# Residual inputs on VectorE in pieces, squares and row rests by products, and a written order at the norm and the routing of a two-layer MoE transformer kernel

## The chip, the cores and the metric

The kernel runs on one core of one Trainium2 chip. The metric is the device time of one execution in microseconds (us). TensorE (PE) does the products, VectorE (DVE), ScalarE (ACT) and GpSimd (POOL) the rest. SyncE (SP) issues nearly all weight transfers on one queue. Each engine takes its own instructions in a fixed order and waits at one until what it needs is there.

## The reference

256 tokens of width 1024 pass through two layers. Cut to what matters here:

```python
# layer 1: modulated conformer convolution, then a mixture of experts
y = depthwise_conv(glu(h @ w_in + b_in), w_dw)        # 31 taps
y = silu(layernorm(y, ln_g, ln_b)) @ w_out
x = x + gate1 * y
h = rmsnorm(x) * (1 + scale2) + shift2
x = x + gate2 * hier_moe(h)                           # 32 experts, top 2 of one group of 8
x = rmsnorm(x, final_g)
# layer 2: latent attention, layer norm, block attention, final norm
x = layernorm(x + mla(x), ln_g, ln_b)
...
```

The residual input of the latent attention is therefore the normalized row times `final_g` (called x3 here), and that of the block attention is the normalized row times `ln_g` plus `ln_b` (called x4).

## The kernel before, in words

Tokens stand in two tiles of 128 rows (t = 0, 1), channels in eight chunks of 128 (k). A product with float32 accuracy is made of single-pass ones: a value is split into a rounded part (suffix h) and a rest (suffix l), hi by ACT and lo by DVE (`split`, L282 and L283), and three products are summed.

**Convolution and its norm (L457 to L585).** DVE does the taps of four chunks (L411), PE those of the other four as products with small blocks. After each chunk `chunk_stats` takes off a first estimate of the mean (`mp`), squares on ACT, and adds up the squares of six chunks on POOL into `ssum` (L484); the chunks' values go into `asum` (L471), also on POOL. PE makes the mean per token (`pms`) and the sums per token (`pst`) of these by products with a column of 1/1024. From `pst` come variance, the power -0.5 on POOL (L565), a diagonal `rst`, and its spread over all partitions by a product (`prs`). Each chunk is then centred (L573), scaled (L577), passed through SiLU (L579, `ysl`) and split into `yh`, `yl` for the out-projection `po`. Beside it lie the two halves of the first gate: products `adp`, copied out by ACT as `ads` (L297). The out-projection's weights are split into `wh`, `wl` by ACT and DVE.

**Routing (L683 to L780).** The rows `x2` get their norm factor `rs2`; a rounded part `xh` and a rest `xl` are made of them, the rest of one tile by POOL, that of the other by DVE (L745). DVE finds the experts by a chain of small operations, two exponentials of it on ACT. `pw` are products that keep PE busy and whose result is not used. A gather by products (`acc`) starts the experts. The 32 experts' weights come in pieces of 2 MB (`in_moe`), issued by SP as buffers become free.

**Layer 2.** In the latents' stage POOL multiplies the rows by `final_g` (L1455, two operations of 128x1024), while DVE splits weights. After the layer norm `to_channels` turns `x4n` into channels chunk by chunk: PE transposes (`pt`), ACT or DVE scales (`xf`), ACT rounds (`xh`), DVE takes the rest (`xl`, 128x128). POOL makes x4 at the same time (L1546 and L1547, four operations of 128x1024). Then `values(0)`, and eight key chunks: PE makes a chunk, `rope_t` splits it (`cqh`), turns it by a product, DVE and POOL multiply by sine and cosine (`t`, `raw`), and DVE adds them (`kn`).

Where a pool's scheduler places an instruction, it goes by due times; `keep_in_program_order` and `pe_order` pin an instruction to its place in the source among the others so pinned on its engine, and `issue_after` places the ones inside it behind a given one.

Of the kernel before, what the change touches and what calls it, by code (L numbers as in the profile page):

```python
# [6 lines left out]
F32 = mybir.dt.float32  # L7
# [41 lines left out]
LN_DVE = ()  # L49
# [29 lines left out]
WARM_R = 2, 3  # L79
# [106 lines left out]
def build(tc, A, out, dbg=None, stop=None):  # L186
# [79 lines left out]
    crep = pre.tile([P, KD, 32], F32, name="crep")  # L266
    modc = const.tile([P, 48], F32, name="modc")
# [21 lines left out]
    def ada_part(psp, pool, ps=None):  # L289
        w = W.get()  # L290
        pt = psp.tile([P, 512], F32, name="adp", tag="adp")
        for k in range(KD):
            j = k % 4
            mm(pt[32 * j:32 * j + 32, :], crep[:, k, :], w[:, k, :], k < 4, k >= 4)
        if ps is None:
# [169 lines left out]
    ssum = wk.tile([P, T], F32, name="ssum", tag="ssum", bufs=1)  # L465
# [11 lines left out]
    def chunk_stats(i, k):  # L477

        nc.vector.tensor_sub(y[:, k, :], y[:, k, :], mp)
        if i < 6:  # L480
            s2 = ssum if i == 0 else wk.tile([P, T], F32, name="s2", tag="sg")
            nc.scalar.activation(s2, y[:, k, :], AF.Square)
            if i:
                nc.gpsimd.tensor_add(ssum, ssum, s2)  # L484
            if i >= PRE:
                running_sum(i, asum, y[:, k, :], PRE)
        if i == 5:
            mm(pms, mean1, asum, True, False)
            products(2, asum, False)
            products(0, ssum, False)  # L490
        elif i > 5:
            s2 = wk.tile([P, T], F32, name="s2", tag="sg")
            nc.scalar.activation(s2, y[:, k, :], AF.Square)
# [24 lines left out]
    for group in CONV:  # L518
# [4 lines left out]
        for k in group:  # L523
# [27 lines left out]
    def rows_of(w, k):  # L551

        wh = wsp.tile([P, 512], F32R, name="wh", tag="wh")
        wl = wsp.tile([P, 512], F32R, name="wl", tag="wl")
        split(wh, wl, w[:, k, :])
        return wh, wl

    wo = W.peek(wo_at - W.nget)
    wos = [rows_of(wo, k) for k in range(WSP)]
    del wo  # L560

    nc.vector.tensor_copy(st[:, 0:4], pst)
    nc.vector.tensor_mul(st[:, 2:4], st[:, 2:4], st[:, 2:4])
    nc.vector.scalar_tensor_tensor(st[:, 0:2], st[:, 0:2], EPS, st[:, 2:4], op0=OP.add, op1=OP.subtract)
    nc.gpsimd.tensor_tensor(out=st[:, 0:2], in0=st[:, 0:2], in1=expn[:, 0:2], op=OP.pow)  # L565
    rst = wk.tile([P, T], F32, name="rst", tag="mp", bufs=1)
    for t in range(NT):
        nc.vector.tensor_scalar(rst[:, P * t:P * t + P], ident, st[:, t:t + 1], None, op0=OP.mult)
# [3 lines left out]
    for k in range(KD):  # L572
        nc.vector.tensor_sub(y[:, k, :], y[:, k, :], pms)  # L573
    yh = xy.tile([P, KD, T], F32R, name="yh", tag="up")
    yl = xt.tile([P, KD, T], F32R, name="yl")
    for k in range(KD):
        nc.vector.tensor_mul(y[:, k, :], y[:, k, :], prs)  # L577
        ys = wk.tile([P, T], F32, name="ysl", tag="ht")
        nc.scalar.activation(ys, y[:, k, :], AF.Silu, scale=vec[:, V_LNG + k:V_LNG + k + 1],  # L579
                             bias=vec[:, V_LNB + k:V_LNB + k + 1])  # L580
        if k in LN_DVE:
            nc.vector.tensor_copy(yh[:, k, :], ys)
            nc.vector.tensor_sub(yl[:, k, :], ys, yh[:, k, :].bitcast(F32))
        else:
            split(yh[:, k, :], yl[:, k, :], ys)  # L585
# [83 lines left out]
    for h in range(2):  # L669
        ada_row(5, h, g2b[:, 512 * h:512 * h + 512], psA)  # L670
# [42 lines left out]
    def first_max(val, n, mx, oh, tmp):  # L713
# [31 lines left out]
    tc.keep_in_program_order(nc.vector.scalar_tensor_tensor(  # L745
        xl2[:, 0, :], x2[:, 0, :], rs2[:, 0:1], xh2[:, 0, :].bitcast(F32), op0=OP.mult, op1=OP.subtract))
# [5 lines left out]
    for i in range(WARM_R[1]):  # L752
        mm(pw[:, 0:256], ident, g2b[:, 0:256], True, True)
    del pw
# [47 lines left out]


    ig = mo.tile([P, P + 4 * E], F32R, name="ig")
    nc.scalar.copy(ig[:, 2 * E:2 * E + P], ident)
    for t in range(NT):
        c = (P + 2 * E) * t
        nc.scalar.copy(ig[:, c:c + E], G[:, t, :])
        nc.vector.tensor_sub(ig[:, c + E:c + 2 * E], G[:, t, :], ig[:, c:c + E].bitcast(F32))
# [463 lines left out]
    def rope_t(dst, pin, rot, cos, sin):  # L1273
# [289 lines left out]
    for m in range(8):  # L1563
        rope_t([kn[:, m, :]], chunk_t(KD, xh, xl), r64, tab(T_COSB), tab(T_SINB))
# [124 lines left out]
```

## Time and profile before

| | |
|---|---|
| time, median of 3 runs (lowest to highest) | 946.23 us (945.17 to 946.7) |
| the profiled execution | 945.95 us |
| its span, first to last instruction | 944.3 us |
| mean granted clock of PE, as a share of full speed | 0.981 |
| PE busy | 869.0 us (92%) |
| DVE busy | 526.6 us (56%) |
| ACT busy | 361.2 us (38%) |
| POOL busy | 58.2 us (6%) |
| read from HBM | 287.34 MB |

The shares are averages over the whole span. Between the profiled execution and its span lie 1.65 us. Read by stages, there are stretches in which PE waits and stretches in which the transfers are what ends last; the rows further down show both.

### The profile page before, as it was taken

How to read it: one execution, taken by the hardware profiler on the slowest of the kernel's cores; microseconds unless marked ns; L12 is line 12 of the kernel's file. 1: busy time of each engine (PE TensorE's matmuls, PEld its weight loads, DVE VectorE, ACT ScalarE, POOL GpSimd, SP SyncE). 2: the span in 40 equal slices, each digit the busy share in tenths (PEclk: the TensorE clock that was granted, in tenths of full speed). 3: DMA queues.
4: the chain of work that ended last, by engine and by line, in shares of the span. 5: the costliest groups of instructions: out<-in, count | busy, mean ns of one | idle time of the engine just before them, and what ended most of it. 6: DMA issues, size and time to landing. Idle time of an engine off the chain costs nothing. (4 is left out here: it accounts for less than half of the span.)

```text
span 944.3 us, 15434 instructions
## 1 busy us (share of the span) xinstructions
PE 869.0 (92%) x6227; PEld 609.6 (65%) x6227; DVE 526.6 (56%) x1243; ACT 361.2 (38%) x788; POOL 58.2 (6%) x62
## 2 busy tenths in 40 slices
PE   4899879899999999999699999878999996999996
PEld 1597346665565555656356555538988874988975
DVE  2699965623343333334223342357777868758876
ACT  1455645412122121212012121145766735655761
POOL 0000210100000000000000000003100004110112
PEclk9899989999999999999899999999999998999998
DMA  9994968789999999999999999974432441624211
GB/s 372 411 389 191 406 249 317 323 362 426 427 427 428 426 427 426 427 426 430 422 428 425 426 429 425 425 311 159 170 140 91 179 178 45 255 102 179 90 45 45
DMA packets 23580, 289.44 MB, mean 307 GB/s; under 512 B 2736, under 2 KB 3408, under 8 KB 6096
## 3 DMA queue, kind: packets, MB, share of 16 engines
q1 hardware_dynamic: 21872, 282.29, 72.4%
q10 hardware_dynamic: 1632, 6.11, 1.8%
q8 instruction: 51, 0.84, 0.4%
q14 instruction: 25, 0.20, 0.1%
HBM read 287.34 MB, written 1.05 MB: 305 GB/s over the span
## 5 line engine op out<-in xcount | busy, mean ns | idle before, releaser
L197 PE MATMUL pgu<-w,xg 128*64 128x256 f32 x2048 | 233.5, 381 | 4.2 <-DMA w<-in_moe 4.2
L197 PEld LDWEIGHTS pgu<-w,xg 128*64 128x64 f32 x2048 | 145.6, 137 | 90.1 <-issue 20.8
L197 PE MATMUL pys<-w,hTe 128*64 128x512 f32 x512 | 116.1, 594 | 5.4 <-DMA w<-in_moe 2.5
L283 DVE TENSOR_TENSOR sl<-w,sh 128x1024 fp32r<-128x1024 f32 (+2 forms) x82 | 98.0, 1204 | 20.4 <-ACT sh L282 19.2
L282 ACT CAST sh<-w 128x1024 fp32r<-128x1024 f32 (+2 forms) x82 | 81.4, 1001 | 48.9 <-PE pj L197 46.0
L1012 DVE SCALAR_TENSOR_TENSOR yt<-pys,gs,g2b 64x512 f32<-64x512 f32 x64 | 48.0, 750 | 87.2 <-PE pys L197 86.2
L282 ACT CAST yh<-yt 64x512 fp32r<-64x512 f32 x64 | 39.6, 618 | 138.9 <-DVE yt L1012 137.3
L197 PE MATMUL pj<-xh,sh 128*128 128x256 f32 x304 | 86.6, 285 | 0.1
L197 PE MATMUL pj<-xl,sh 128*128 128x256 f32 x304 | 85.5, 281 | 0.0
L197 PE MATMUL pj<-xh,sl 128*128 128x256 f32 x304 | 85.3, 281 | 0.0
L197 PEld LDWEIGHTS pys<-w,hTe 128*64 128x64 f32 x512 | 36.2, 137 | 65.9 <-issue 54.5
L854 DVE TENSOR_TENSOR hid<-pgu,hid 128x256 f32<-128x256 f32 x32 | 13.6, 425 | 97.2 <-ACT hid L853 97.2
L853 ACT ACTIVATE hid<-pgu 128x256 f32<-128x256 f32 x32 | 12.3, 385 | 125.8 <-PE pgu L197 119.7
L197 PEld LDWEIGHTS pj<-xh,sh 128*128 128x128 f32 x304 | 57.1, 188 | 2.2 <-issue 1.6
L197 PEld LDWEIGHTS pj<-xl,sh 128*128 128x128 f32 x304 | 57.0, 188 | 1.8 <-issue 1.7
L197 PEld LDWEIGHTS pj<-xh,sl 128*128 128x128 f32 x304 | 57.1, 188 | 0.8 <-issue 0.8
L411 DVE SCALAR_TENSOR_TENSOR y<-up,wdw,y 128x256 f32<-128x256 f32 x120 | 54.9, 513 | 0.1
L283 DVE TENSOR_TENSOR yl<-yt,yh 64x512 fp32r<-64x512 f32 x64 | 44.0, 687 | 2.2 <-ACT yh L282 0.2
L197 PE MATMUL pu<-hh,wh 128*128 128x256 f32 x128 | 37.4, 292 | 2.7 <-ACT wh L282 2.7
L283 DVE TENSOR_TENSOR wl<-w,wh 128x512 fp32r<-128x512 f32 x48 | 33.2, 702 | 12.0 <-ACT wh L282 10.5
L282 ACT CAST wh<-w 128x512 fp32r<-128x512 f32 x48 | 29.3, 620 | 27.5 <-PE pu L197 20.4
L862 DVE COPY hTe<-pth 128x256 f32<-128x256 f32 x32 | 13.6, 425 | 44.6 <-PE pth L203 40.1
(343 smaller groups left out, 1579.2 us busy)
## 6 DMA issues: line engine op xcount, KB each, us to landing
w<-in_moe SPq DMA_DIRECT2D x95, 2048.0 KB, 32.0
w<-in_wst SPq DMA_DIRECT2D x32, 2048.0 KB, 8.7
w<-in_wst SPq DMA_DIRECT2D x5, 1152.0 KB, 5.1
w<-in_wst SPq DMA_DIRECT2D x2, 1536.0 KB, 11.2
wb<-in_wbd ACTq DMA_DIRECT2D x4, 512.0 KB, 7.0
w<-in_wst SPq DMA_DIRECT2D x2, 1024.0 KB, 22.6
w<-in_moe SPq DMA_DIRECT2D x4, 512.0 KB, 31.2
x<-in_x SPq DMA_DIRECT2D x1, 1024.0 KB, 11.5
```

The source lines that it names most:

```text
L197: ins = nc.tensor.matmul(o, l, r, start=start, stop=stop)
L282: a = nc.scalar.copy(hi, src)
L283: return a, (eng or nc.vector).tensor_sub(lo, src, hi.bitcast(F32))
L411: nc.vector.scalar_tensor_tensor(y[:, m, :], u, wdw[:, m, k:k + 1], y[:, m, :], op0=OP.mult, op1=OP.add)
L853: nc.scalar.activation(hid, pgu[:, 0:256], AF.Silu)
L854: nc.vector.tensor_mul(hid, pgu[:, 256:512], hid)
L862: nc.vector.tensor_copy(hT, pt.rearrange("p (q j s) -> p q j s", q=2, j=2))
L1012: nc.vector.scalar_tensor_tensor(yt[r, :], pys[r, :], gs[r, e % 2:e % 2 + 1], g2b[r, 512 * j:512 * j + 512], op0=OP.mult, op1=OP.mult)
```

## The change

Five things change in the code.

1. The squares of the first six chunks of the convolution are no longer summed on POOL. Each chunk's squares go into `pst` by two products of one column each, as those of the last two chunks did.
2. At the layer norm the order of ACT's and DVE's work is written down: first the weight splits, then centring, copies and table load, then the second half of the gate's products ahead of `prs`, and a SiLU, a cast and a rest per chunk.
3. At the routing the products without use are removed. `x2` is no longer scaled in place. The rests `xl` come from PE: a diagonal of the norm factors times the rows, minus the rounded rows, copied out by ACT in four pieces of 128x512. One of the two roundings stands between the two exponentials on ACT.
4. `ig`, the table of gate values for the scatter, is built behind the first gather.
5. x3 and x4 are made by DVE in pieces of 128x512, four behind the latents' query chunks and eight behind the key chunks' splits.

```diff
     def chunk_stats(i, k):
-        nc.vector.tensor_sub(y[:, k, :], y[:, k, :], mp)
+        sub = nc.vector.tensor_sub(y[:, k, :], y[:, k, :], mp)
+        s2 = wk.tile([P, T], F32, name="s2", tag="sg")
+        sq = nc.scalar.activation(s2, y[:, k, :], AF.Square)
...
         if i < 6:
-            s2 = ssum if i == 0 else wk.tile([P, T], F32, name="s2", tag="sg")
-            nc.scalar.activation(s2, y[:, k, :], AF.Square)
-            if i:
-                nc.gpsimd.tensor_add(ssum, ssum, s2)
+            products(0, s2, False)
...
-    wos = [rows_of(wo, k) for k in range(WSP)]
+    wos = [rows_of(wo, k, True) for k in range(WSP)]
...
+    centre(0, 1, 2, 3)
+    gate1.append(wk.tile([P, 512], F32, name="ads", tag="ads"))
+    keep(nc.scalar.copy(gate1[1], gate1.pop(0)))
+    keep(nc.scalar.activation(small[:, 8:9], small[:, 0:1], AF.Silu))
...
+    centre(4, 5)
+    gate1.append(ada_part(psA, wk))
     rst = wk.tile([P, T], F32, name="rst", tag="mp", bufs=1)
...
     mm(prs, ones, rst, True, True)
-    gate1.append(ada_part(psA, wk))
...
-    pw = psU.tile([P, 512], F32, name="pw", tag="pu")
-    for i in range(WARM_R[0]):
-        mm(pw, ident, g2b[:, 0:512], True, True)
...
-    nc.scalar.mul(x2[:, 1, :], x2[:, 1, :], rs2[:, 1:2])
-    split(xh2[:, 1, :], xl2[:, 1, :], x2[:, 1, :], nc.gpsimd)
-    nc.scalar.activation(xh2[:, 0, :], x2[:, 0, :], AF.Identity, scale=rs2[:, 0:1])
+    dr = wk.tile([P, NT, P], F32, name="dr", tag="mp", bufs=1)
+    for t in range(NT):
+        keep(nc.scalar.mul(dr[:, t, :], ident, rs2[:, t:t + 1]))
+    keep(nc.scalar.activation(xh2[:, 0, :], x2[:, 0, :], AF.Identity, scale=rs2[:, 0:1]))
+
+    def rest_of_rows(j):
+        for t in range(NT):
+            c = slice(512 * j, 512 * j + 512)
+            pw = psU.tile([P, 512], F32, name="pw", tag="pu")
+            mm(pw, dr[:, t, :], x2[:, t, c], True, False)
+            mm(pw, nident, xh2[:, t, c], False, True)
+            keep(nc.scalar.copy(xl2[:, t, c], pw))
...
-    tc.keep_in_program_order(nc.vector.scalar_tensor_tensor(
-        xl2[:, 0, :], x2[:, 0, :], rs2[:, 0:1], xh2[:, 0, :].bitcast(F32), op0=OP.mult, op1=OP.subtract))
...
     for i in range(CQ_FIRST, 6):
-        latent_q(i)
-    with tc.issue_after(kv_norm.ins):
-        for t in range(NT):
-            nc.gpsimd.tensor_mul(x2[:, t, :], x2[:, t, :], fg[:, 0, :])
+        with tc.issue_after(latent_q(i).ins):
+            t, c = (i - CQ_FIRST) // 2, slice(512 * (i % 2), 512 * (i % 2) + 512)
+            nc.vector.tensor_mul(x2[:, t, c], x2[:, t, c], fg[:, 0, c])
...
-    for t in range(NT):
-        nc.gpsimd.tensor_mul(x4[:, t, :], x4n[:, t, :], gb[:, 0, :])
-        nc.gpsimd.tensor_add(x4[:, t, :], x4[:, t, :], gb[:, 1, :])
...
+    def x4_part(m, after):
+
+        with tc.issue_after(after.ins):
+            t, c = m // 4, slice(512 * (m // 2 % 2), 512 * (m // 2 % 2) + 512)
+            if m % 2:
+                nc.vector.tensor_add(x4[:, t, c], x4[:, t, c], gb[:, 1, c])
+            else:
+                nc.vector.tensor_mul(x4[:, t, c], x4n[:, t, c], gb[:, 0, c])
...
     for m in range(8):
-        rope_t([kn[:, m, :]], chunk_t(KD, xh, xl), r64, tab(T_COSB), tab(T_SINB))
+        x4_part(m, rope_t([kn[:, m, :]], chunk_t(KD, xh, xl), r64, tab(T_COSB), tab(T_SINB)))
```

On PE, at the end of the convolution, this is what stands there before; `s` are squares of single chunks, `adp` the gate's products:

```order
L197 MATMUL pms<-asum,mean_86 128x256
L197 MATMUL pst<-mean_86,asum 128x1 x2
L197 MATMUL pms<-y,mean_86 128x256
L197 MATMUL adp<-w,crep 32x512 x3
L197 MATMUL pms<-y,mean_86 128x256
L197 MATMUL pst<-mean_86,ssum 128x1 x2
L197 MATMUL pst<-mean_86,y 128x1 x2
L197 MATMUL pst<-mean_86,s_1300 128x1 x2
L197 MATMUL pst<-mean_86,y 128x1 x2
L197 MATMUL pst<-mean_86,s_1385 128x1 x2
L197 MATMUL prs<-rst,ones 128x256
L197 MATMUL adp<-w,crep 32x512 x8
```

The same place of PE after the change:

```order
L195 MATMUL adp<-w,crep 32x512
L195 MATMUL pms<-asum,mean_86 128x256
L195 MATMUL pst<-mean_86,s_1298 128x1 x2
L195 MATMUL pst<-mean_86,asum 128x1 x2
L195 MATMUL pms<-y,mean_86 128x256
L195 MATMUL pst<-mean_86,y 128x1 x2
L195 MATMUL adp<-w,crep 32x512 x4
L195 MATMUL pst<-mean_86,s_1307 128x1 x2
L195 MATMUL adp<-w,crep 32x512 x3
L195 MATMUL pms<-y,mean_86 128x256
L195 MATMUL pst<-mean_86,y 128x1 x2
L195 MATMUL pst<-mean_86,s_1390 128x1 x2
```

Seven instead of three `adp` of the first gate half stand between the first `pms` and the last `pst`; behind the last row come the eight `adp` of the second half and only then `prs`.

On ACT, at the norm, before (`s` squares, `ads` the copies of the gate halves):

```order
L493 ACTIVATE s_1300<-y 128x256
L282 CAST wh<-w 128x512
L297 COPY ads<-adp 128x512
L493 ACTIVATE s_1385<-y 128x256
L282 CAST wh<-w 128x512 x3
L579 ACT_TABLE_LOAD
L579 ACTIVATE ysl<-y,vec 128x256 x2
L297 COPY ads<-adp 128x512
L282 CAST yh<-ysl 128x256 x2
```

The same place of ACT after the change:

```order
L483 ACTIVATE s_1307<-y 128x256
L483 ACTIVATE s_1390<-y 128x256
L282 CAST wh<-w 128x512 x4
L573 COPY ads<-adp 128x512
L574 ACT_TABLE_LOAD
L574 ACTIVATE small<-small 128x1
L300 COPY ads<-adp 128x512
L594 ACTIVATE ysl<-y,vec 128x256 x2
L597 CAST yh<-ysl 128x256
L594 ACTIVATE ysl<-y,vec 128x256
```

The second `ads` copy now stands ahead of the SiLUs instead of between them and the casts, and all four `wh` casts stand ahead of the first `ads` copy.

On DVE, in the key chunks' stage, before:

```order
L283 TENSOR_TENSOR sl<-w,sh 128x1024
L283 TENSOR_TENSOR cqh<-raw,cqh 128x256
L1260 TENSOR_TENSOR t_7156<-pr,tbl 128x256
L1265 TENSOR_TENSOR kn<-raw,t_7156 128x256
L283 TENSOR_TENSOR sl<-w,sh 128x1024
L283 TENSOR_TENSOR cqh<-raw,cqh 128x256
```

And after:

```order
L283 TENSOR_TENSOR cqh<-raw,cqh 128x256
L1571 TENSOR_TENSOR x_7028<-x4n,rows 128x512
L1277 TENSOR_TENSOR t_7173<-pr,tbl 128x256
L1282 TENSOR_TENSOR kn<-raw,t_7173 128x256
L283 TENSOR_TENSOR sl<-w,sh 128x1024
L283 TENSOR_TENSOR cqh<-raw,cqh 128x256
L1569 TENSOR_TENSOR x_7028<-x_7028,rows 128x512
L1277 TENSOR_TENSOR t_7214<-pr,tbl 128x256
L1282 TENSOR_TENSOR kn<-raw,t_7214 128x256
L283 TENSOR_TENSOR sl<-w,sh 128x1024
```

Behind each `cqh` split one piece of x4 has come in, by turns a product and a sum, eight in all.

## Rows read from the trace of the kernel before

**Rows 1.** The windows: us, busy time of each engine, PE's clock, DMA share, GB/s

```profile
190.00:192.00 2.00, 2.00 (x22) 1.31 (x20) 0.00 (x0) 0.28 (x1) 0.00 (x0) 1.00 0.06 16
...
194.00:402.00 208.00, 205.44 (x1520) 121.85 (x1518) 75.81 (x167) 43.03 (x87) 0.00 (x0) 1.00 1.01 427
```

**Rows 2.** Timeline: start, length, engine; SP's issue and PE's wait for weights

```profile
192.02 3.78 SPq L168 DMA_DIRECT2D w<-in_moe  x2
...
616.54 1.94 PE L197 MATMUL pys<-w,hTe 128*64 128x512 f32 x8 [1.18 <-DMA w<-in_moe]
```

**Rows 3.** Timeline of DVE's taps beside one sum of squares on POOL

```profile
115.35 3.01 DVE L411 SCALAR_TENSOR_TENSOR y<-up,wdw,y 128x256 f32<-128x256 f32 x5
...
116.08 0.81 POOL L484 TENSOR_TENSOR ssum<-ssum,s 128x256 f32<-128x256 f32 x1
...
117.50 0.87 DVE L411 SCALAR_TENSOR_TENSOR y<-up,wdw,y 128x256 f32<-128x256 f32 x2
```

**Rows 4.** Timeline of PE from the convolution's end to the out-projection

```profile
124.29 1.06 PE L197 MATMUL adp<-w,crep 128*32 128x512 f32 x6
...
132.37 1.19 PE L197 MATMUL prs<-rst,ones 128*128 128x256 f32 x2 [4.26 <-DVE rst L568]
...
133.49 3.58 PE L197 MATMUL adp<-w,crep 128*32 128x512 f32 x16
...
138.09 0.49 PE L197 MATMUL po<-wh,yh 128*128 128x512 f32 x1 [0.65 <-ACT yh L282]
```

**Rows 5.** Timeline of DVE and ACT in the same stretch

```profile
128.55 1.89 DVE L283 TENSOR_TENSOR wl<-w,wh 128x512 fp32r<-128x512 f32 x3
...
134.06 1.10 ACT L579 ACTIVATE ysl<-y,vec 128x256 f32<-128x256 f32 x2 [4.90 <-DVE y L577]
...
137.15 0.59 ACT L297 COPY ads<-adp 128x512 f32<-128x512 f32 x1 [1.99 <-PE adp L197]
...
137.63 0.71 ACT L282 CAST yh<-ysl 128x256 fp32r<-128x256 f32 x2
```

**Rows 6.** The windows of the same stretch, columns as in the first group

```profile
132.00:136.00 4.00, 3.63 (x14) 1.10 (x18) 3.94 (x14) 1.10 (x2) 0.00 (x0) 0.50 0.00 0
```

**Rows 7.** Timeline of the routing: POOL and DVE

```profile
177.09 2.38 POOL L283 TENSOR_TENSOR xl<-x,xh 128x1024 fp32r<-128x1024 f32 x1 [3.67 <-ACT xh L282]
...
177.45 2.10 DVE L717 TENSOR_TENSOR t<-em,r 128x64 f32<-128x64 f32 x1
...
181.52 1.28 DVE L745 SCALAR_TENSOR_TENSOR xl<-x,rs,xh 128x1024 fp32r<-128x1024 f32 x1
```

**Rows 8.** Timeline of the latents' stage: POOL and PE

```profile
646.82 4.75 POOL L1455 TENSOR_TENSOR x<-x,rows 128x1024 f32<-128x1024 f32 x2 [0.30 <-issue]
...
652.88 0.42 PE L1450 MATMUL ptk<-cst,kr 128*96 128x128 f32 x2 [2.49 <-DVE kr L1447]
```

**Rows 9.** The windows of the latents' query chunks and of one key chunk

```profile
653.00:667.00 14.00, 13.60 (x114) 13.00 (x113) 9.85 (x14) 9.45 (x19) 3.66 (x4) 1.00 0.41 152
...
812.00:815.05 3.05, 3.05 (x29) 3.05 (x29) 2.32 (x4) 1.79 (x4) 0.82 (x2) 1.00 0.98 419
```

**Rows 10.** Timeline of `to_channels` after the layer norm: POOL and DVE

```profile
785.66 4.72 POOL L1546 TENSOR_TENSOR x<-x4n,rows 128x1024 f32<-128x1024 f32 x2 [2.13 <-PE pj L197]
...
785.81 4.72 DVE L283 TENSOR_TENSOR xl<-xf,xh 128x128 fp32r<-128x128 f32 x2
...
790.96 4.26 DVE L283 TENSOR_TENSOR xl<-xf,xh 128x128 fp32r<-128x128 f32 x2
...
795.65 0.28 DVE L283 TENSOR_TENSOR xl<-xf,xh 128x128 fp32r<-128x128 f32 x1
```

**Rows 11.** Timeline of POOL and DVE at one key chunk

```profile
814.88 0.75 POOL L1261 TENSOR_TENSOR raw<-raw,tbl 128x256 f32<-128x256 f32 x1 [2.23 <-DVE cqh L283]
...
815.87 0.43 DVE L1265 TENSOR_TENSOR kn<-raw,t 128x256 f32<-128x256 f32 x1
...
817.35 0.42 DVE L283 TENSOR_TENSOR cqh<-raw,cqh 128x256 fp32r<-128x256 f32 x1
```

More of the change, by code (lines that the diff above doesn't have):

```diff
@@ L549, in build, with rows_of @@
     nc.scalar.dma_start(g1b, A["vecs"][V_AB + 16:V_AB + 24, :].rearrange("r c -> (r c)").unsqueeze(0).to_broadcast([P, D]))
-    def rows_of(w, k):
+    def rows_of(w, k, in_order=False):
         wh = wsp.tile([P, 512], F32R, name="wh", tag="wh")
         wl = wsp.tile([P, 512], F32R, name="wl", tag="wl")
-        split(wh, wl, w[:, k, :])
+        for a in split(wh, wl, w[:, k, :]):
+            if in_order:
+                keep(a)
         return wh, wl
+    keep = tc.keep_in_program_order
@@ L558, in build, with centre @@
     wo = W.peek(wo_at - W.nget)
-    wos = [rows_of(wo, k) for k in range(WSP)]
+    wos = [rows_of(wo, k, True) for k in range(WSP)]
     del wo
-    nc.vector.tensor_copy(st[:, 0:4], pst)
-    nc.vector.tensor_mul(st[:, 2:4], st[:, 2:4], st[:, 2:4])
-    nc.vector.scalar_tensor_tensor(st[:, 0:2], st[:, 0:2], EPS, st[:, 2:4], op0=OP.add, op1=OP.subtract)
+    def centre(*ks):
+        for k in ks:
+            keep(nc.vector.tensor_sub(y[:, k, :], y[:, k, :], pms))
+    centre(0, 1, 2, 3)
+    gate1.append(wk.tile([P, 512], F32, name="ads", tag="ads"))
@@ L565, in build @@
+    keep(nc.scalar.copy(gate1[1], gate1.pop(0)))
+    keep(nc.scalar.activation(small[:, 8:9], small[:, 0:1], AF.Silu))
+    keep(nc.vector.tensor_copy(st[:, 0:4], pst))
+    keep(nc.vector.tensor_mul(st[:, 2:4], st[:, 2:4], st[:, 2:4]))
+    keep(nc.vector.scalar_tensor_tensor(st[:, 0:2], st[:, 0:2], EPS, st[:, 2:4], op0=OP.add, op1=OP.subtract))
     nc.gpsimd.tensor_tensor(out=st[:, 0:2], in0=st[:, 0:2], in1=expn[:, 0:2], op=OP.pow)
+    centre(4, 5)
+    gate1.append(ada_part(psA, wk))
     rst = wk.tile([P, T], F32, name="rst", tag="mp", bufs=1)
@@ L567, in build @@
     for t in range(NT):
-        nc.vector.tensor_scalar(rst[:, P * t:P * t + P], ident, st[:, t:t + 1], None, op0=OP.mult)
+        keep(nc.vector.tensor_scalar(rst[:, P * t:P * t + P], ident, st[:, t:t + 1], None, op0=OP.mult))
     prs = psA.tile([P, T], F32, name="prs", tag="adr")
     mm(prs, ones, rst, True, True)
-    gate1.append(ada_part(psA, wk))
-    for k in range(KD):
-        nc.vector.tensor_sub(y[:, k, :], y[:, k, :], pms)
+    centre(6, 7)
     yh = xy.tile([P, KD, T], F32R, name="yh", tag="up")
@@ L575, in build @@
     yl = xt.tile([P, KD, T], F32R, name="yl")
[L576 to L585, printed above, removed]
+    yss = []
@@ new lines, in build @@
+    for k in range(KD + 1):
+        if k < KD:
+            keep(nc.vector.tensor_mul(y[:, k, :], y[:, k, :], prs))
+            yss.append(wk.tile([P, T], F32, name="ysl", tag="ht"))
+            keep(nc.scalar.activation(yss[k], y[:, k, :], AF.Silu, scale=vec[:, V_LNG + k:V_LNG + k + 1],
+                                      bias=vec[:, V_LNB + k:V_LNB + k + 1]))
+        if k:
+            keep(nc.scalar.copy(yh[:, k - 1, :], yss[k - 1]))
+            keep(nc.vector.tensor_sub(yl[:, k - 1, :], yss[k - 1], yh[:, k - 1, :].bitcast(F32)))
@@ L588, in build @@
+    del yss
     x2T = y
@@ L669, in build @@
     for h in range(2):
-        ada_row(5, h, g2b[:, 512 * h:512 * h + 512], psA)
+        ada_row(5, h, g2b[:, 512 * h:512 * h + 512], psA, ("adr", "adp")[h])
     dump("x2", x2)
@@ L751, in build @@
     nc.vector.scalar_tensor_tensor(posp, pp, 1.0, oh1, op0=OP.add, op1=OP.mult)
-    for i in range(WARM_R[1]):
-        mm(pw[:, 0:256], ident, g2b[:, 0:256], True, True)
-    del pw
+    rest_of_rows(1)
     dump("posp", posp)
@@ L942, in build @@
         gather(*nxt, range(2 * q, 2 * q + 2), 4 * CAP, acc[q // 2][q % 2])
+    ig = mo.tile([P, P + 4 * E], F32R, name="ig")
+    nc.scalar.copy(ig[:, 2 * E:2 * E + P], ident)
+    for t in range(NT):
+        c = (P + 2 * E) * t
+        nc.scalar.copy(ig[:, c:c + E], G[:, t, :])
+        nc.vector.tensor_sub(ig[:, c + E:c + 2 * E], G[:, t, :], ig[:, c:c + E].bitcast(F32))
     oh, xg = nxt
@@ L1276, in rope_t @@
         nc.scalar.copy(raw, pin)
-        rh = rl = None
+        rh = rl = last = None
         if rot.dtype == F32R:
@@ L1280, in rope_t @@
             rh, rl = (cqh[:, 2 * spare[0] + i] for i in range(2))
-            split(rh, rl, raw)
+            last = split(rh, rl, raw)[1]
         ropes.append((dst, raw, rh, rl, rot, cos, sin))
@@ L1284, in rope_t @@
             rope_end()
+        return last
     mask = tab(T_MASK)
```

50 lines of the change are left out of this document (24 added, 26 removed).

## The prediction

> **What bounds the kernel now.** The page puts PE at 92% of the span, so I looked first for the stretches where it isn't the limit. The windows of the experts' stage show the largest: from 194 us PE is busy nearly throughout, but the DMA share is 1.01 at 427 GB/s, and near the end PE stands still for weights [rows 1, 2]. In that stage the transfers end last; the reader should note that SP issues the first piece after the routing's ones at 192.02, when PE has begun the experts, so the whole train of transfers moves with the front of the kernel, and a gain ahead of it isn't lost in it. I then read PE's timeline for its idle times outside that stage. Three places stand out. At the convolution's norm PE waits 4.26 for `rst`, runs the gate's products at half clock, and waits again, up to the first `po` at 138.09 [rows 4, 6]. In the latents' stage it waits 2.49 for DVE's `kr` [rows 8]. In `to_channels` after the layer norm DVE's short rests last 2.1 to 2.4 us, one after another [rows 10].
>
> The last two have one cause. A rest of 128x128 takes 0.28 alone, but two take 4.72 while POOL's two operations of 128x1024 take 4.72 beside them: each DVE operation with two inputs in SBUF lasts as long as the POOL operation [rows 10]. The same shows in the routing, where 64 columns on DVE take 2.10 beside POOL's 2.38 [rows 7], and at the taps, where five take 3.01 beside POOL and two take 0.87 after it [rows 3].
>
> **The change part by part.**
>
> *Squares by products.* At 0.435 each the five taps would be 2.2, so the two POOL sums beside them cost 0.8, some 0.4 each. Four of the five sums of squares lie beside taps: 1.6 us of DVE. Against it, four more of the gate's pairs now stand between the first `pms` and the last `pst`: eight instructions at 1.06/6 are 1.4 us of PE [rows 4]. I set part 1 at 0 (bounds -0.8 and +1.6).
>
> *Norm.* From the last `pst` to the first `po` three things leave the path. The three weight splits that lay between DVE's small steps, 1.89 [rows 5]. Half of `prs`, which took 1.19 at half clock: 0.6 [rows 4, 6], because the second gate half now keeps PE busy until then. And ACT's wait for that gate half: the SiLUs end at 135.16, the casts to `yh` begin only at 137.63, since `ads` stands between and waits for the 3.58 us of `adp`: 2.5 [rows 4, 5]. The eight pairs themselves now lie beside DVE's centring and POOL's power; at full speed they need 1.4 to 1.8. Together 5.0. As the first `po` comes earlier, it then meets ACT's SiLU, cast and weight cast per chunk, of which PE now waits for some: I take 0.5 off. **4.5** (bounds 2.1, below, to 5.5).
>
> *Routing.* DVE loses the hold of 1.9 and its own rest of 1.28, 3.2 at most [rows 7]. Given back: a rounding of 1024 columns now stands before the second exponential on ACT, for which I take DVE's 1.28 for as many columns. And the second group of rests stands on PE between the position products and the gather: two float32 products, of two passes each, and two single-pass ones. At 0.49 a pass, as `po` shows for 512 columns [rows 4], that is 2.9, in place of six passes of half that width without use, 1.5: 1.4 more. 3.2 - 1.3 - 1.4 = **0.5** (bounds 0 and, if all but the hold cancels, 1.9). `ig` behind the gather lies beside PE's products: 0; without that cover its five small operations, below 2 us, would take that half microsecond and more.
>
> The third of the pieces SP issues at the routing now waits for the last product of the rests instead of POOL's sum. The two ahead of it keep the queue busy for about 10 us (2 MB at 427 GB/s is 4.9 each [rows 1]). The rests should be done by then, so 0.
>
> *x3.* POOL's two operations of 2.38 go [rows 8], and with them the hold that made `kr` late: the wait of 2.49 goes. Four DVE pieces come in. A piece has 512 columns and two SBUF inputs like the weight split of 0.63 [rows 5]; four are 2.5 us, and DVE has 4.15 free in the 14 us of query chunks [rows 9]. **2.4** (bounds 1.5, should a piece or two meet POOL's sums there, and 2.5).
>
> *x4, the gain.* Four long rests of 4.72 and 4.26 for two become 0.28 each: 8.98 - 1.12 = 7.9 [rows 10]. DVE's chain is what ends last there; a bit more comes where a rest overlaps its neighbour, less where ACT's share of the chain ends last instead. **8.0** (bounds 7.0 and 9.0, a microsecond each way).
>
> *x4, the cost.* Eight pieces of 0.63 go into the key chunks, each behind a `cqh` split. By busy time there is room: DVE is busy 2.32 of a chunk's 3.05 [rows 9]. But the order matters. POOL's product of `raw` waits for that same split [rows 11], so piece and product want to start together, and by the holds above they go one after the other: 0.61 + 0.07 + 0.75 before `kn` can start. Before, `kn` started 0.99 behind POOL's start at 814.88, or 1.06 behind the split; now 1.43 to 1.5. From `kn`'s start to the end of the next split are 1.90 [rows 11]. That makes a cycle of 3.4 against PE's 3.05, and PE's turn of the key (`pr`) waits for the split. Seven cycles at 0.35: 2.4 lost. Were the pieces hidden, it is 0; were each added in full with POOL's 0.82, it is (2.32 + 0.63 + 0.82 - 3.05) x 8 = 5.8. I take **-2.4**, since three places show holds of this kind [rows 3, 7, 10].
>
> A rule speaks on this point. The Trainium skill (SBUF — State Buffer, "SBUF: two separate sides") calls the pair of ports that DVE and GpSimd share an exclusive lock, held for the whole instruction, with the loser blocked; the rows agree, 4.72 beside 4.72. The Trainium skill (Perfetto Trace Analysis, "Optimizing Scalar/DVE Operations") concludes that moving work between those two "might not help". By that rule this change would lose among the query and key chunks what it gains in `to_channels` and the latents. The trace does not bear that out in full: the POOL product among the key chunks is 0.75 long and not 2.4.
>
> *Sum.* 4.5 + 0.5 + 2.4 + 8.0 - 2.4 = 13.0. Against the profiled execution, 945.95 (span 944.3 and 1.65 around it), that gives 932.95; the median of the runs is 946.23, 0.03% away. I say 932.9.
>
> **The rivals.**
>
> *Pieces hidden.* POOL's product slips in beside DVE's `t`, or PE runs ahead enough that a late split never stops it. For it: PE is never idle in that window. Against: DVE's wait there is for PE itself, so there is little in hand. 930.6.
>
> *Key chunks bound by DVE.* The full 5.8, by further collisions, in place of 2.4: 936.4.
>
> *The clock falls again at the norm.* PE still waits about 2 us for the first `yh`. In the window at 132 the granted clock is 0.50 [rows 6]; at that level `prs` and the eight pairs stay at 1.19 and 3.58 [rows 4] and now stand on the path: 0.6 + 1.8 come back, 935.4. For it: before, the fall followed such a wait. Against: PE now works through the wait for the power.
>
> *The front's gain is swallowed.* If the transfers are bound by the pieces issued in the routing and not by the one at 192.02, an earlier PE meets the same last weight: the 5.0 of the front goes, 938.0. Against it: the DMA share is 0.06 in the two microseconds before 192 [rows 1], so nothing is queued ahead of that piece.
>
> *Slower.* Each DVE piece is held like the rests were, at p us. The gain without pieces is 15.4; cover is 0.73 in each of eight chunks and 1.04 in each of four [rows 9], so the pieces cost 12p - 10.0. It decides from p = 2.1; at 2.36, half of 4.72, it is 18.3 and the time 948.9. Against: no POOL operation of more than 0.82 is left there.
>
> *It does nothing.* The collisions between the two engines only move, so that x3 and x4 lose among the query and key chunks what they gain elsewhere (each piece at about 1.7 by the sum just made), and the front is swallowed: 946.0. Against: the same cover as above. This is the case of the Trainium skill's sentence in Perfetto Trace Analysis that was quoted.
>
> **How the numbers follow.** The forecast with its own range of 930.9 to 934.7 gets 0.44; hidden pieces (928.0 to 930.9) 0.22; the DVE bound 0.08; the clock 0.09; the front swallowed 0.06; slower 0.03; nothing 0.03; more gain than any term allows for 0.05. From 928.0 to 936.6 stand four of these cases with 0.83, and the range ends there. Two executions of this kernel differ by up to 0.2% (1.9 us), which is what a measurement can tell from no change; by the cases, faster 0.94, same 0.03, slower 0.03.
>
> **What would show it.** Right: the casts to `yh` follow the first SiLU without a wait for `ads`; the first `in_moe` piece behind the routing's is issued about 5 us before 192.02; `ptk` follows without its 2.49; rests in `to_channels` at 0.28; in the key chunks a repeated PE wait for DVE's `cqh` of about 0.35, and POOL's `raw` beginning only when the piece ends. Wrong: PE without a wait among the key chunks (pieces hidden), a wait there of 0.7 (DVE bound), the last weight at the same time as before (front swallowed), half clock again behind `prs`, or pieces of over 1 us.

## The result

The changed kernel takes 932.0 us (median of 4 runs, 930.75 to 933.45) against 945.75, a ratio of 0.9854 with an interval of 0.9837 to 0.9872. The forecast was 932.9 (928.0 to 936.6). A second set of five runs of the same code (e12 below) has a median of 934.89 against 946.11, a ratio of 0.9877 (0.9854 to 0.9900), so 932 to 935 is what the change gives. Single runs of the kernel before lie between 944.2 and 949.5, further apart than the 1.9 us that the forecast took, so medians less than 2 us apart are not told apart here, and small terms are read from the traces. The profiled execution took 931.65, its span is 930.0, which is 14.3 less than before.

The sum came out well, the terms did not: the front gave 1.3 where 5.0 were forecast, layer 2 gave 13.0 where 8.0 were (1.0 and 11.3 in the profile of e12). Both ends can be read in the rows of the profile after.

PE's timeline from the convolution's end to the out-projection, to be held against [rows 4]:

```profile
123.81 0.70 PE L195 MATMUL pms<-asum,mean 128*128 128x256 f32 x2
...
126.10 1.07 PE L195 MATMUL adp<-w,crep 128*32 128x512 f32 x8
...
129.52 0.59 PE L195 MATMUL pst<-mean,s 128*128 128x1 f32 x4
130.03 1.92 PE L195 MATMUL adp<-w,crep 128*32 128x512 f32 x16
132.69 0.67 PE L195 MATMUL prs<-rst,ones 128*128 128x256 f32 x2 [0.73 <-DVE rst L583]
133.25 0.44 PE L195 MATMUL pl<-zeros,ones 128*128 128x72 f32 x2
135.29 0.59 PE L195 MATMUL po<-wh,yh 128*128 128x512 f32 x1 [1.59 <-ACT yh L597]
```

The wait of 4.26 for `rst` is down to 0.73 and `prs` runs at full clock, 0.67 for 1.19. But `prs` starts no earlier than before (132.69 for 132.37): the sums end later. The first `po` comes 2.8 earlier. Then the windows show a stretch at half clock (a granted clock of 0.50, the lower of PE's two levels) behind PE's wait of 1.59:

```profile
136.00:138.00 2.00, 2.00 (x5) 1.57 (x6) 0.78 (x3) 1.03 (x3) 0.00 (x0) 0.50 1.10 467
```

At the routing the hold is gone: the 64 columns that took 2.10 take 0.23 [rows 7]. What ends last now is seen in DVE's timeline:

```profile
176.16 0.23 DVE L736 TENSOR_TENSOR t<-em,r 128x64 f32<-128x64 f32 x1
...
179.77 0.23 DVE L770 SCALAR_TENSOR_TENSOR posp<-pp,oh 128x64 f32<-128x64 f32 x1 [0.81 <-PE pp L195]
182.03 1.39 DVE L797 TENSOR_SCALAR oh<-cst,posp 128x64 fp32r<-128x64 f32 x8 [2.04 <-PE pw L195]
```

The one-hots `oh` wait 2.04 for the last rest product `pw`. Their tile is allocated right after the pools that hold the rows and the diagonal are closed, which is why I take it that they wait for the memory; the row names PE's `pw` as what ended the wait. The gather starts at 182.92 for 184.24.

SP's first issue behind the routing's moved with it, and the experts still end on transfers (SP's and PE's timelines; [rows 2] before):

```profile
190.79 0.33 SPq L166 DMA_DIRECT2D w<-in_moe  x1
...
615.33 1.94 PE L195 MATMUL pys<-w,hTe 128*64 128x512 f32 x8 [1.33 <-DMA w<-in_moe]
```

192.02 became 190.79, and the wait for weights at 616.54 stands at 615.33: 1.2 each. What the front gains passes through the experts' stage one to one, as forecast.

In layer 2, DVE's timeline in `to_channels` and POOL's and DVE's at one key chunk ([rows 10, 11] before):

```profile
779.75 0.28 DVE L283 TENSOR_TENSOR xl<-xf,xh 128x128 fp32r<-128x128 f32 x1
...
780.95 0.71 DVE L283 TENSOR_TENSOR xl<-xf,xh 128x128 fp32r<-128x128 f32 x2
...
796.94 0.42 DVE L283 TENSOR_TENSOR cqh<-raw,cqh 128x256 fp32r<-128x256 f32 x1
797.27 0.68 DVE L1571 TENSOR_TENSOR x<-x4n,rows 128x512 f32<-128x512 f32 x1
797.50 1.07 POOL L1278 TENSOR_TENSOR raw<-raw,tbl 128x256 f32<-128x256 f32 x1 [20.02 <-DVE cqh L283]
797.89 0.42 DVE L1277 TENSOR_TENSOR t<-pr,tbl 128x256 f32<-128x256 f32 x1
798.60 0.43 DVE L1282 TENSOR_TENSOR kn<-raw,t 128x256 f32<-128x256 f32 x1 [0.28 <-POOL raw L1278]
798.94 1.22 DVE L283 TENSOR_TENSOR sl<-w,sh 128x1024 fp32r<-128x1024 f32 x1
800.08 0.42 DVE L283 TENSOR_TENSOR cqh<-raw,cqh 128x256 fp32r<-128x256 f32 x1
```

The rests are at 0.28. In the key chunk the collision that was forecast is there: POOL's product lasts 1.07 instead of 0.75 (1.06 or 1.07 in all eight chunks) and `kn` waits for it. But from split to split it is 3.14, not 3.4.

### The profile page after: what moved, and what is told of

The parts are those of the page before. It is cut to its first block, busy times and chain, and to the rows that moved or that the text cites. A ratio compares the mean times of both kernels' runs of the same rounds, so it can differ in the third digit from the quotient of the medians.

```text
span 930.0 us, 15479 instructions
## 1 busy us (share of the span) xinstructions
PE 871.4 (94%) x6249; PEld 611.3 (66%) x6249; DVE 516.4 (56%) x1255; ACT 362.2 (39%) x794; POOL 39.7 (4%) x50
## 5 line engine op out<-in xcount | busy, mean ns | idle before, releaser
L283 DVE TENSOR_TENSOR sl<-w,sh 128x1024 fp32r<-128x1024 f32 (+2 forms) x82 | 95.6, 1173 | 18.8 <-ACT sh L282 17.7
L414 DVE SCALAR_TENSOR_TENSOR y<-up,wdw,y 128x256 f32<-128x256 f32 x120 | 52.5, 484 | 0.1
```

What stands on the lines that cost most here:

```text
L283: return a, (eng or nc.vector).tensor_sub(lo, src, hi.bitcast(F32))
L414: nc.vector.scalar_tensor_tensor(y[:, m, :], u, wdw[:, m, k:k + 1], y[:, m, :], op0=OP.mult, op1=OP.add)
```

## The experiments

For comparison I read the same starts from PE's timeline of each kernel: the first `pms`, `prs`, the first `po`, the gate's rows `adr` in the routing, the first gather product `acc`, the first transposes `pt<-cst,x` of layer 2, `ptk`, the first and last transposes of `x4n`, and the end of the span. Times in us. All kernels were timed against the kernel before, whose median in those runs was 945.2 to 946.1.

| | pms | prs | po | adr | acc | layer 2 | ptk | x4n first | last | end | median |
|---|---|---|---|---|---|---|---|---|---|---|---|
| before | 122.79 | 132.37 | 138.09 | 173.44 | 184.24 | 633.54 | 652.88 | 780.57 | 799.18 | 944.27 | 945.75 |
| changed | 123.81 | 132.69 | 135.29 | 172.15 | 182.92 | 632.29 | 647.67 | 774.52 | 784.38 | 929.99 | 932.0 |
| e1 | 122.93 | 132.51 | 137.71 | 173.10 | 183.88 | 633.15 | 648.54 | 775.32 | 785.21 | 930.71 | 932.82 |
| e2 | 123.51 | 130.87 | 133.47 | 170.43 | 181.20 | 630.79 | 647.56 | 774.75 | 784.61 | 930.14 | 931.26 |
| e3 | 123.86 | 132.74 | 135.34 | 172.29 | 182.89 | 632.13 | 649.10 | 776.01 | 785.88 | 931.37 | 933.72 |
| e4 | 124.47 | 133.35 | 135.95 | 172.93 | 183.69 | 633.08 | 649.87 | 777.00 | 795.59 | 940.17 | 942.12 |
| e5 | 123.19 | 130.56 | 133.16 | 169.76 | 183.00 | 632.48 | 647.88 | 775.01 | 784.89 | 930.38 | 932.46 |
| e6 | 121.65 | 129.85 | 133.01 | 169.92 | 180.69 | 630.02 | 645.43 | 772.06 | 781.93 | 927.47 | 930.0 |
| e7 | 124.28 | 133.16 | 135.76 | 172.72 | 183.49 | 632.96 | 649.93 | 777.05 | 792.75 | 938.83 | 940.59 |
| e8 | 124.35 | 131.72 | 134.32 | 171.27 | 181.68 | 632.62 | 647.99 | 774.83 | 784.70 | 930.29 | 931.3 |
| e9 | 122.68 | 130.05 | 132.65 | 168.44 | 179.04 | 628.54 | 643.92 | 771.01 | 780.88 | 926.45 | 928.94 |
| e10 | 123.79 | 134.54 | 140.23 | 175.58 | 186.38 | 636.08 | 651.47 | 778.06 | 787.92 | 933.40 | 936.94 |
| e11 | 123.55 | 130.92 | 133.52 | 170.47 | 181.05 | 630.35 | 647.28 | 774.41 | 784.27 | 929.91 | 931.58 |
| e12 | 124.00 | 132.88 | 135.48 | 172.45 | 183.22 | 632.50 | 649.39 | 776.56 | 786.43 | 931.96 | 934.89 |

The first `pms` alone varies by more than 2 us between kernels whose code is the same up to there (e2, e5, e6 and e8: 121.65 to 124.35), so differences of starts within one kernel are read, not starts.

**e1: part 5 alone.** Only the x3 and x4 hunks of the diff, on the kernel before.

> The kernel before with part 5 alone: x3 and x4 by DVE in pieces, the front (convolution, norm, routing) as it was. Theory 1, from the two traces (the first in_moe issue behind the routing moved by only 1.2 us, and the rest of the shift came in layer 2): the pieces are worth nearly all of the change, 12 to 13 us, some 933 us, and the gather stays at about 184.2. Theory 2, the terms as predicted (front 5.0, layer 2 8.0): 938 us.

932.82, ratio 0.9874 (0.9853 to 0.9896); gather at 183.88. Theory 1. The twelve pieces carry the change; the other four parts together don't show in the time. x3 and x4 were not tried apart here; e4 takes out x4 alone.

**e10: the squares by products on top of e1.** Its diff is that of `chunk_stats`.

> As e1 (the kernel before with the pieces of x3 and x4), with part 1 as well: the squares by products. Theory 1: the products cost 2 us on PE at the convolution's end: the first pms starts 0.5 to 1 us later than 122.93, and from it to prs takes about 1 us longer than the 9.58 of e1; time about 934.5. Theory 2: the cost seen in the changed kernel comes from the written order alone; then both stay within 0.3 us and the time is that of e1, 932.8.

936.94, ratio 0.9913 (0.9891 to 0.9935). From `pms` to `prs` 10.75 for e1's 9.58, and `prs` 2.03 later, of which 0.86 lie at the first `pms`, within what that start varies by. Theory 1 for the stage: between `pms` and `prs` part 1 costs 1.2 us without the written order, and 1.64 from `pms` to the gather. The median is 2.4 above the theory's time; the profiled execution, at 935.05, was the shortest of the four, and the record does not show where the others lost more.

**e2: the squares back on POOL in the changed kernel.**

```diff
-            products(0, s2, False)
+            if i:
+                nc.gpsimd.tensor_add(ssum, ssum, s2)
...
+                products(0, ssum, False)
```

> The changed kernel with the squares of the convolution summed on POOL again, all else as changed. Theory 1: the five pairs of one-column products lie on PE, whose queue is what ends last in the convolution, so without them the first pms starts 1 us or more earlier than 123.81 and the time is about 931, although DVE's taps take 2 us longer again. Theory 2: DVE's taps end last there; then pms starts later than 123.81 and the time is 933 or more.

931.26, ratio 0.9841 (0.9822 to 0.9859). From `pms` to `prs` 7.37, against 8.88 in every kernel with the products and the written order (changed, e3, e4, e7, e12). Theory 1 for the cause, but not for the place: the first `pms` comes only 0.30 earlier than 123.81, and the cost that can be read, 1.4 to the gather, lies behind it. The two medians are too close to tell the kernels apart. The groups of DVE's lines in the convolution show why its gain doesn't count: before,

```profile
L411 DVE SCALAR_TENSOR_TENSOR y<-up,wdw,y 128x256 f32<-128x256 f32 x70 | 32.4, 529 | 0.0
L479 DVE TENSOR_TENSOR y<-y,mp 128x256 f32<-128x256 f32 x8 | 3.2, 424 | 1.7 <-ACT y L434 1.7
L307 DVE TENSOR_REDUCE modc<-adc 128x4 f32<-128x16 f32 x4 | 0.7, 166 | 0.0
```

and changed:

```profile
L414 DVE SCALAR_TENSOR_TENSOR y<-up,wdw,y 128x256 f32<-128x256 f32 x70 | 30.4, 492 | 0.0
L481 DVE TENSOR_TENSOR y<-y,mp 128x256 f32<-128x256 f32 x7 | 2.8, 415 | 3.2 <-ACT y L437 3.2
L310 DVE TENSOR_REDUCE modc<-adc 128x4 f32<-128x16 f32 x4 | 0.7, 168 | 1.4 <-PE adc L308 1.4
```

The taps got 2.0 us, where the prediction gave them 1.6. DVE then waits 2.9 more, 1.4 for PE itself and 1.5 for ACT's `y`, which copies what PE has made.

**e11: the written norm order and the pieces alone.** The changed kernel with e2's edit and the routing of before.

> The changed kernel without part 1 and part 3: squares on POOL, the routing of before; the written norm order, ig and the pieces stay. Theory 1: from pms to prs 7.4 us as in e2, and the gather where e2 has it, 10.6 to 10.8 behind the gate's rows, so the time is that of e2, about 931.3. Theory 2: rests by products are worth what was predicted for them, so it is 0.5 us or more slower than e2.

931.58, ratio 0.9851 (0.9833 to 0.9870). 7.37 from `pms` to `prs`; from `adr` to the gather 10.58, in e2 10.77. Theory 1. From `pms` to the gather it takes 57.50, in e1 60.95, so the norm order (with `ig`) is worth 3.45: 4.81 at the first `po` (9.97 behind `pms` for 14.78), of which some is given back in the out-projection. Against e3, which differs by part 1 only, the gather is 1.53 nearer to `pms`.

**e3: the routing of before in the changed kernel.**

> The changed kernel with the routing of before: rests by POOL and DVE, rows scaled in place, products without use. Theory 1: the rests by products give back at the gather what the chain on DVE gains, because the first one-hot on DVE waits for the last rest product on PE (2.04 us in the trace of the changed kernel). From the end of the norm's sums to the gather takes 11.9 us in both traces, so the time stays at 932 within 0.5 us. Theory 2, the predicted term: 0.5 us slower or more, with the gather 0.5 to 1.9 us later.

933.72, ratio 0.9875 (0.9852 to 0.9897). From `adr` to the gather 10.60 for the changed kernel's 10.77. Theory 1 in the trace: the rests by products are worth nothing. The longer time, which lies between those of the two sets of the changed kernel, is that of the start of layer 2 (16.97 from the transposes to `ptk` for 15.38), which e12 takes up.

**e8: all rests ahead of the position products**, on e2: `rest_of_rows(1)` right behind `rest_of_rows(0)`.

> As e2, with all four rests by products ahead of the position products on PE, instead of two ahead and two behind. Theory 1: in the changed kernel DVE's first one-hot waits 2.04 us for the last rest product; with the products done first that wait goes and the gather comes about 0.5 to 1 us earlier than 181.20, though the position products start 1 us later. Theory 2: the products wait for ACT's copies of their two buffers, the position products start 2 us later and the gather doesn't gain.

931.3, ratio 0.9844 (0.9827 to 0.9861). `adr` to gather 10.41 for e2's 10.77: the wait of `oh` went, the position products came later, 0.4 is left. A half-clock stretch in the gather itself (0.50 from 184 to 186) cost more than that in this execution: from the gather to layer 2 it takes 450.94, in e2 449.59. Undecided, and small.

**e4: x4 on POOL again in the changed kernel.**

> The changed kernel with x4 made by POOL again (four operations of 128x1024 in to_channels), x3 still by DVE. Theory 1: POOL's four operations hold DVE's short rests again and the key chunks lose their pieces: 8.7 back in to_channels, 0.85 off in the key chunks, so about 940 us. Theory 2, as predicted (8.0 and 2.4): 937.6 us. Both expect long rests of 2.1 to 2.4 us and a key chunk of 3.05 instead of 3.15 us.

942.12, ratio 0.9954 (0.9938 to 0.9969). POOL's and DVE's timelines:

```profile
782.10 4.71 POOL L1565 TENSOR_TENSOR x<-x4n,rows 128x1024 f32<-128x1024 f32 x2 [2.14 <-PE pj L195]
782.23 4.74 DVE L283 TENSOR_TENSOR xl<-xf,xh 128x128 fp32r<-128x128 f32 x2
```

The holds are back. From the first to the last transposes of `x4n` it takes 18.59, as before (18.61), against 9.86 with the pieces: 8.7. From there to the end 144.58, against 145.61 with them. So the pieces cost 1.0 behind `to_channels` and bring 8.7 in it. The time lies 2 us above theory 1; the profile has 1.4 more at the start of layer 2 and a `pms` 0.7 later.

**e7: the eight pieces on POOL.** `nc.vector` becomes `nc.gpsimd` in `x4_part`.

> The changed kernel with the eight pieces of x4 made by POOL, in the same places and sizes. Theory 1: what counts is the engine: each piece of about 1.2 us on POOL holds DVE's two-input operations and stands ahead of POOL's own product of raw, so a key chunk takes 3.8 us or more instead of 3.15, and the time is 5 us longer, about 937. Theory 2: what counts is the place, away from to_channels; a piece beside DVE's split costs no more than on DVE, and the time is that of the changed kernel, 932.

940.59, ratio 0.9936 (0.9912 to 0.9961). Slower, but not where I expected it:

```profile
781.97 2.57 POOL L1571 TENSOR_TENSOR x<-x4n,rows 128x512 f32<-128x512 f32 x2 [1.96 <-ACT xf L1207]
...
782.28 2.41 DVE L283 TENSOR_TENSOR xl<-xf,xh 128x128 fp32r<-128x128 f32 x2
```

A place in the program is no wait. POOL had nothing ahead of the pieces, ran them as soon as `x4n` was there, and held DVE's rests at some 1.2 each: 15.70 for the transposes of `x4n`, between 9.86 and 18.59. It bears out that the length of POOL's operation is the length of the hold; it says nothing on a POOL piece among the key chunks, which was not tried.

**e5: PE kept busy at the norm**, on e2: behind `pl`, ahead of `po`,

```diff
+    pf = psU.tile([P, 512], F32, name="pf", tag="pu")
+    mm(pf, ident, g1b[:, 0:512], True, True)
+    mm(pf[:, 0:256], ident, g1b[:, 0:256], True, True)
```

> As e2 (squares on POOL), with two float32 products without use (512 and 256 columns) behind pl, where PE waits 1.59 us for the first yh before the out-projection. Theory 1: the granted clock stays at full through the first twelve po, so these take about 3.3 us, as in the kernel before, and not the 4.85 of e2, and the gather comes 1 to 1.5 us earlier than 181.20. Theory 2: the chain of DVE's and ACT's written order (rest, product, SiLU, cast) sets the pace of the first chunks, so PE waits instead and the gather moves by less than 0.5 us.

932.46, ratio 0.9865 (0.9846 to 0.9885). At the out-projection theory 1: the granted clock is 1.00 in the windows from 132 to 142 us, 0.57 in e2's from 134 to 138. But the gather is at 183.00, 1.8 later than in e2. The windows of e5 at the routing:

```profile
168.00:170.00 2.00, 2.00 (x12) 2.00 (x12) 0.33 (x3) 1.52 (x3) 0.69 (x1) 0.53 0.00 0
170.00:172.00 2.00, 2.00 (x4) 0.97 (x5) 1.73 (x11) 0.00 (x0) 0.00 (x0) 0.50 0.61 131
172.00:174.00 2.00, 2.00 (x9) 1.65 (x8) 1.76 (x9) 0.44 (x1) 0.00 (x0) 0.50 0.94 393
```

In this profile the half-clock stretch stands at the routing instead, behind shorter waits of PE between the last transposes of the rows, and costs more there. Neither theory had that.

**e6: DVE's products two chunks ahead, three SiLU buffers**, on e2.

> As e2, with DVE's products by prs written two chunks ahead of the rests instead of one, and three buffers for the SiLU's output instead of two. Theory 2 of e5: the written order's loop of about 1.8 us per chunk goes down to ACT's 1.5, so the second and third chunk's casts come earlier and the gather 0.5 to 1 us earlier than 181.20. Theory 1: PE at half clock sets the pace, nothing changes (gather within 0.3 us).

930.0, ratio 0.9845 (0.9814 to 0.9877). No gain from the edit can be read: its `pms` is the earliest of all, ahead of the edit, and a half clock around `prs` cost 1.4 (from `pms` to `po` 11.36 for 9.97). From `adr` to the gather it is 10.77, as in e2. From `po` to `adr` 36.91 for 36.96. Theory 1.

**e9: three fills.** e5, a product of 256 columns between the last transposes of the rows, and four instead of three products without use behind the experts (`WARM`).

> As e5 (squares on POOL, products without use ahead of the out-projection), with one more such product of 256 columns between the last transposes of the out-projection's rows, and four instead of three behind the experts. Theory 1: a half-clock stretch follows PE's waits at four places in turn (norm, routing, gather, start of layer 2); with all four waits shortened no such stretch stands between 130 and 190 us or at 634, and the span is 2 to 3 us below that of e5, about 928. Theory 2: it only moves once more, to the next wait, and the span stays at 930.

928.94 (928.49 to 929.67), ratio 0.9825 (0.9808 to 0.9843). Theory 1. The granted clock is 1.00 in every window read at the four places; two of them:

```profile
134.00:138.00 4.00, 4.00 (x16) 2.53 (x15) 3.16 (x7) 3.35 (x8) 0.00 (x0) 1.00 0.73 307
...
168.00:172.00 4.00, 4.00 (x26) 3.04 (x26) 3.08 (x17) 2.70 (x6) 0.20 (x1) 1.00 0.59 184
```

Its span is 926.45, shorter than the theory's 928, and its five runs all lie below those of both kernels. Held against e2, which has the same squares and no fill, the span is 3.7 shorter: 0.8 of it ahead of the first `pms`, where the code is the same, 1.3 from there to the gather (56.36 for 57.69), and 1.4 at the start of layer 2. The last is not shown to come from the fourth product: e5 and e6 have the same 15.4 there without it.

**e12: the changed kernel again.**

> The changed kernel once more, unaltered, for a second profile of the same code. Theory 1: the start of layer 2 takes one of two lengths by where the granted clock falls, 15.4 us from the first transposes to ptk (as in the first profile) or 16.8 to 17.0 (as in the kernel before without its wait), and the rest of the terms stays: 8.88 from pms to prs, 10.8 from the gate's rows to the gather, 9.86 in to_channels. Theory 2: the 15.4 belongs to the changed code, and the other stages vary as much. The time should again be 932 within 1 us, so that e9 stays some 3 us below it.

934.89, ratio 0.9877 (0.9854 to 0.9900). Theory 1 for the stages: 8.88, 10.77 and 9.87 once more, but 16.89 from the transposes of layer 2 to `ptk`, where the first profile had 15.38. The window there in the first profile,

```profile
634.00:636.00 2.00, 1.62 (x14) 1.45 (x13) 2.00 (x6) 1.63 (x4) 0.00 (x0) 1.00 0.61 203
```

and in the second:

```profile
634.00:636.00 2.00, 1.63 (x8) 1.38 (x9) 1.88 (x6) 1.37 (x4) 0.00 (x0) 0.66 0.65 207
```

In the first the clock had fallen from 627 to 631 already, beside the products without use, and was back. The thirteen profiles without the wait at `ptk` have one of two lengths here, 15.4 (seven) or 16.8 to 17.0 (six). In the six long ones the clock falls to half within this stage, at 632.6 to 635.4; in the seven short ones it fell earlier, at 627 to 631 (four), or not at all (e5, e6, e9). The time is 2.9 us above the 932 that I expected, where I had allowed 1.

## Why the prediction was right

The range was met by luck as much as by the sum: its errors had both signs, 3.7 too much for the front and 5.0 too little for layer 2. Of the signs named ahead, four came: `yh` without a wait for `ads`, `ptk` without its wait, rests at 0.28, and POOL's product held by the piece. Two did not: the first `in_moe` issue moved by 1.2 and not by 5, and PE shows no wait for `cqh` among the key chunks. Term by term, in us:

| term | forecast | measured | read from |
|---|---|---|---|
| squares by products | 0 (-0.8 to 1.6) | -1.4 to -1.6 behind the first `pms`; ahead of it about -1, not sure | `pms` to gather: changed and e2, e3 and e11, e10 and e1 |
| norm | 4.5 (2.1 to 5.5) | 3.5 | `pms` to gather: e1 and e11, e10 and e3 |
| routing | 0.5 (0 to 1.9) | -0.2 | `adr` to gather, e2 and e11 |
| x3 | 2.4 (1.5 to 2.5) | 2.45 | layer 2 to `ptk`: 19.34 before, 16.89 in e12 |
| x4 in `to_channels` | 8.0 (7.0 to 9.0) | 8.75, of it 7.5 by the holds | first to last transposes, 18.61 and 9.86 |
| x4 in the key chunks | -2.4 (-5.8 to 0) | -0.5 to -1.0 | last transposes to the end: before or e4, and changed |

*Squares.* The step that failed: "I set part 1 at 0", taking the 1.6 on DVE against 1.4 of gate products on PE. DVE's part was right to 0.4, and the four gate pairs took 1.0 (126.10 to 127.09). But the five pairs of one-column products themselves were put at nothing. They stand in PE's stream as well, at 0.45 each by the starts of such pairs one after the other (in e2's tail they start at 126.90, 127.35, 127.80 and 128.24), and PE's stream feeds ACT, whose `y` DVE waits for. In e2 ACT copies the last `y` of the convolution 2.23 ahead of the first `pms`, which then waits for POOL:

```profile
121.28 0.48 ACT L437 ACTIVATE y<-py,vec 128x256 f32<-128x256 f32 x1 [3.73 <-PE py L195]
...
123.51 0.70 PE L195 MATMUL pms<-asum,mean 128*128 128x256 f32 x2 [0.80 <-POOL asum L474]
```

In the changed kernel it is copied only 0.47 ahead of the `pms` at 123.81:

```profile
123.34 0.47 ACT L437 ACTIVATE y<-py,vec 128x256 f32<-128x256 f32 x1 [3.73 <-PE py L195]
```

So DVE could not cash in its gain, and the prediction should have had the cost without the gain. How much lies ahead of the first `pms` stays unsure: it starts at 124.04 in the mean of the six kernels with the products and at 123.08 in that of the eight without, and the latter spread over 2.7.

*Norm.* The mechanism held: no wait of `yh` for `ads`, `prs` at full clock, first `po` 4.8 nearer to the first `pms` (e1 to e11; 5.0 forecast). The loss behind it was put at 0.5 and is 1.4. It was named as a rival, "the clock falls again at the norm", but at the wrong place: not `prs` and the gate's products lay in it, those ran at 0.67 and 1.92, but most of the first twelve `po`, which took 4.57 for 3.11.

*Routing.* The forecast had 1.9 gained on DVE and ACT and 1.4 lost on PE. In the two profiles `posp` comes 1.65 earlier behind `adr` (7.62 for 9.27): the hold went, DVE's own rest of 1.28 had mostly lain beside the position products and gave little, and ACT's rounding cost a wait of 0.62 and not 1.28. From `posp` to the gather it takes 1.62 longer (3.15 for 1.53), for the first one-hots wait for the last rest product: the chain on DVE, its hold gone, ends in a wait of 2.04. The term was a difference of two nearly equal numbers, and it came out at nothing.

*x3.* Right to 0.1, read from the stage, as no run has x3 alone. The first profile shows 1.5 more, which is where its clock fell and not the change: the kernel before and e12 both have 0.50 from 636 to 638, so these two are compared.

*x4.* The gain was 0.75 larger, and the surplus is not the holds. From DVE's `xf` ahead of the first long rest to the one behind the last it takes 9.85 before (785.48 to 795.33) and 2.35 after (779.42 to 781.77): 7.5, for 7.9 forecast. From there to the last transposes it takes 3.85 before and 2.61 after. PE had waited up to 2.05 at a time beside the holds, and then ran at half clock. The windows before and after:

```profile
796.00:799.00 3.00, 3.00 (x9) 2.26 (x9) 1.90 (x6) 2.81 (x8) 0.00 (x0) 0.50 0.00 0
```

```profile
780.00:784.00 4.00, 3.48 (x16) 2.28 (x16) 3.21 (x11) 3.54 (x11) 0.00 (x0) 1.00 0.15 50
```

e4 repeats it, with 3.82 and a clock of 0.50 from 792 to 795. So 1.2 of the gain came by the clock, which the forecast did not have. The cost was mis-sized: the cycle of 3.4 set the piece behind the end of the split and POOL's product behind the end of the piece. In the rows the piece starts 0.33 behind the split's start, 0.09 before its end, and POOL's product ends 0.62 behind the piece, not 0.82. That makes 3.14; from the first `pr` on seven chunks take 18.73 for 18.17, 0.08 a chunk. The collision stands, and PE gives way to it, but by 0.6 in all, in a step from `pr` to the next product that grew from 0.12 to 0.20. That is nearer to the rival "Pieces hidden" than to the forecast.

The Trainium skill (Perfetto Trace Analysis, "Optimizing Scalar/DVE Operations") says of moving work between DVE and GpSimd that it "might not help". Here it did help: 8.7 gained against 1.0 lost. What decided is which of the two held the other, and for how long: a POOL operation of 2.36 beside rests of 0.28, or a piece of 0.68 beside a product of 0.75.

## What to carry to other kernels

Where short operations on DVE take as long as a POOL operation that runs beside them, give POOL's work to DVE in pieces behind the stage's critical chain; it paid nine to one here although DVE was the busier engine. Before a gain on one engine is counted, ask which engine feeds it next: 2.0 us off DVE's taps were worth less than nothing, because the same edit lengthened PE's queue ahead of them. And a wait of PE that is shortened must be judged with the clock: in e5 the time taken out at the norm came back at the routing, and in e9, with both places filled, it did not. These are one profile each. In `to_channels` the gain was larger than the holds because the half clock behind them went as well.

## What was not expected of the hardware

The half-clock stretches are not tied to a place in the code. With the wait at the norm filled (e5) the stretch of 0.50 stood at 168 to 174 us and cost some 2.5 from `adr` to the gather (13.24 for 10.77); with three places filled (e9) none was seen at these places. That the fills are the cause is not shown: e9's runs spread over 1.2 us and those of the changed kernel over 2.7 and 4.0, but those of e11, without a fill, over 1.3. At the start of layer 2 the same code has lengths of 15.4 and 16.9. What in PE's waits decides between these was not settled.
